# Attention's output split in place, and two out-projection blocks begun with it in the attention's PSUM banks

## The chip, the cores and the metric

The kernel runs on one core of one Trainium2 chip. The metric is the device time of one execution in microseconds; the median of three runs of the kernel before is 1607.62 us (1607.45 to 1609.95). Engines are named as in the profile: PE is TensorE, with PEld its weight loads, DVE is VectorE, ACT is ScalarE, POOL is GpSimd and SP is SyncE, whose only work here is to issue DMAs. L319 is line 319 of the kernel before.

## The reference, cut to what matters

One layer of a diffusion backbone over 1024 latent tokens (a grid 64 wide), 256 context tokens and model width 1024. Two groups of heads run side by side, and one projection joins them:

```python
px = modulate(rms_norm(x, norm1_w), sh1, sc1) @ w_in
# group A: gated DeltaNet, 4 heads of 128; chunked scans forwards and backwards, 
#          then per-head rms norm * silu(z)
dn_x, _, _ = gated_deltanet(px[..., :DN_IN], ..., s_ctx_f, s_ctx_b)
# group B: 8 heads of 64; softmax over an 8 x 16 window of keys and all context keys,
#          with a learned position bias
na_x = neighborhood_attention(qx, kx, vx, kc, vc, na_rpb, rows)
x = x + g1 * (jnp.concatenate([dn_x, na_x], axis=-1) @ w_out)
x = x + g2 * swiglu(modulate(rms_norm(x, norm2_w), sh2, sc2), w_ffn_in, w_ffn_out)
```

The concatenation matters for the change: the 1024 rows of `w_out` fall into 512 that meet group A's output and 512 that meet group B's, so a product over all of them can be begun with either half.

## The kernel before, in words

Numbers are held as pairs: an fp32 value is a `hi` (cast to the matmul's fp32r form) and a `lo` (the value less `hi`), and a product is three matmuls, hi by hi, lo by hi, hi by lo. Each operand is thus made by a cast on ACT and a subtraction on DVE or POOL. A scheduler sets the order of the instructions on each engine ahead of time, from the program's priorities and the life of its buffers, so the rows of an engine do not follow the lines of the source. An engine takes its rows in order; SP too, so a DMA that waits for its data or its buffer holds all DMAs behind it.

The kernel has four stages. The first, up to about 610 us, projects the input (L389) and prepares the chunk matrices of the scans. The second interleaves scans and attention. `scan` (L1085 to L1137) takes one of 10 chunks of 128 tokens in one direction: matmuls with the state (L1092, L1102), with `y` (L1111), with `at` (L1123) and `kt` (L1128), and DVE and ACT work on `vn`, `oacc`, `vk` in between. Its operands are loaded by `load` at L1065 to L1073, a chunk ahead, into three slots each. Where both directions have passed a chunk, `finish` norms it (L1149 to L1156), transposes it (L1161) and writes group A's part of the operand, `gah` and `gal` (L1164, L1165). Behind every step of a scan, `beside` advances `attention` by 0.72 of a step.

`attention` (L247 to L354) goes through 32 units, 4 pairs of heads by 2 halves of the rows by 4 blocks of columns. A unit takes a PSUM tile `sc` (1536 columns, two of them in turn) and goes: scores (L295), bias and maximum on DVE (L297), exponential on ACT (L300), scaling on DVE (L302), transposes (L307), copy to `pt` on ACT (L310), product with the values (L317), and a copy of the 128x128 result on ACT into `no` (L319). Four units fill a `no` tile, which SP stores in `na_d` in DRAM (L357).

The third stage is the out-projection (L1315 to L1376). `na_d` is read back (L1322) in four tiles of 512 KB, cast on ACT (L1325) and split on DVE (L1326) into `na`. With group A's `gah` and `gal` that makes the operand `parts`, eight pieces of 128 rows. Each of 8 blocks of 128 output columns takes 512 KB of `w_out` (`load_w`: DMA L197, cast L198, split L199), and 48 matmuls of 512 columns (L1349): eight pieces by three products by two halves of the tokens, the pieces of group A first. DVE then adds the result to the residual `x2` (L1334), whose input is loaded at L1344. The weights of block 0 are loaded during the scans already. Beside the blocks runs the background work `late`, the second half of the modulation (16 loads `wad` of 256 KB, L212, each with a DVE step L231 or L233); blocks 6 and 7 go together, at L1371. The fourth stage is the FFN, whose `Stream` loads the first 8 weight tiles `wq` (L1251, 256 KB each) when it is made, ahead of the out-projection, and casts and splits them (L1279, L1280).

Of the kernel before, what the change touches and what calls it, by code (L numbers as in the profile page):

```python
# [20 lines left out]
KT = 8  # L21
# [66 lines left out]
def hybrid(ctx, tc, a, dbg):  # L88
# [62 lines left out]
    vw_d = dram.tile([128, 4, 4, 512], F32, name="vw_d", tag="vw_d")  # L151
    na_d = dram.tile([4, 128, L], F32, name="na_d", tag="na_d")
    y_d = dram.tile([2, NCH, 128, 4, 128], F32, name="y_d", tag="y_d")
# [87 lines left out]

    hs = [slice(h * 128, h * 128 + 128) for h in range(4)]
    attn = ctx.enter_context(ExitStack())
    psum = []

    def attention(nw):
# [31 lines left out]
        def pair(heads, bts, vw, vc, half, cb, out):  # L278
# [34 lines left out]
            for j in range(5):  # L313
                for u, (w0, pt) in enumerate(zip(WIN, pts)):
# [3 lines left out]
                              start=j == 0, stop=j == 4)  # L318
            act.copy(out.rearrange("p (r b c) -> p r b c", r=8, b=4)[:, :, cb],  # L319
                     sc[:, 1280:1408].rearrange("p (r c) -> p r c", r=8))  # L320
            yield 1
# [7 lines left out]
        for n, (hp, half, cb) in enumerate(order):  # L329
            if half == 1 and cb in (0, 2) and hp + 1 < NAH // 2:  # L330
                heads.setdefault(hp + 1, []).append(load(2 * hp + 2 + cb // 2))
                if cb == 0:
                    vcs[hp + 1] = context(hp + 1)
            if cb == 0:
                out = nw.tile([128, 512], F32, name="no", tag="no")
            if old:
                next(old)
            cur = pair(heads[hp], bt, vw, vcs[hp], half, cb, out)
            next(cur)
            if n + 1 < len(order):  # L340
                bt, vw = biases(*order[n + 1]), values(*order[n + 1])
            yield 1
            if old:
                next(old)
                if cb == 0:
                    store(*done)
            if cb == 3:
                done = out, hp, half
            old = cur
            yield 1  # L350
        next(old)
        yield 1
        next(old)
        store(*done)  # L354

    def store(out, hp, half):
        sp.dma_start(na_d[hp, :, half * 512:half * 512 + 512], out)  # L357


    with ExitStack() as bs:  # L360
# [613 lines left out]
        for n in range(2, len(jobs) + 2):  # L974
# [8 lines left out]
            if n == len(jobs) - 1:  # L983
                bg.drain()
                late.close()
                fill = attention(pools(attn, "nw", "left", 2))
                next(fill)
# [52 lines left out]
    ga = [arp.tile([128, 4, L], F32R, name=n, tag=n) for n in ("gah", "gal")]  # L1040

    with ExitStack() as gs:
        sp1 = pools(gs, "sp1", "right")
# [3 lines left out]
        ps = gs.enter_context(tc.tile_pool(name="psg", bufs=1, space=PSUM))  # L1047
        psum.append(ps)
# [122 lines left out]
        def beside(n):  # L1171
            count[0] += n
            while count[0] >= 1:
                count[0] -= 1
                next(fill, 0)

        for d in range(2):
            load(d, ORDER[d][0])
        for i in range(NCH):
            if i + 1 < NCH:  # L1180
                for d in range(2):
                    load(d, ORDER[d][i + 1])
            live = [scan(d, ORDER[d][i]) for d in range(2)]
            while live:
# [11 lines left out]
    middle.close()  # L1196
    load_w = weights(wp)
    shift(ctx, "pad", "left", 8)
# [7 lines left out]
    rs = nrm.tile([128, L], F32, name="rs", tag="rs")  # L1206
    ps = ctx.enter_context(tc.tile_pool(name="psf", bufs=8, space=PSUM))

    def bank(name="ps"):
        return ps.tile([128, 512], F32, name=name, tag="ps")  # L1210

# [104 lines left out]
    with ExitStack() as os_:  # L1316
        nap = pools(os_, "nap", "right")
        nxt = load_w(a["w_out"][0], lo_engine=dve)
        na = []
        for k in range(4):  # L1320
            raw = wp.tile([128, KT, 132], F32, name="wraw", tag="wraw", bufs=2)[:, :, :128]
            sp.dma_start(raw, na_d[k].rearrange("p (i t) -> p i t", t=128))  # L1322
            n = nap.tile([128, 2, L], F32R, name=f"na{k}", tag=f"na{k}")
            n8 = n.rearrange("p h (i t) -> p h i t", t=128)
            act.copy(n8[:, 0], raw)  # L1325
            dve.tensor_tensor(n8[:, 1], raw, n8[:, 0].bitcast(F32), OP.subtract)  # L1326
            na.append(n)
        parts = [[x[:, k] for k in range(4)] + [n[:, i] for n in na] for i, x in enumerate(ga)]
        late = Background()
# [11 lines left out]

        for b in range(KT - 2):
            w, nxt = nxt, load_w(a["w_out"][b + 1], lo_engine=dve)
            sp.dma_start(x2[:, b], a["xcT"][b, :, CT:])  # L1344
            outs = [bank(), bank()]
            for k in range(KT):
                for j, (wi, xi) in enumerate(((0, 0), (0, 1), (1, 0))):
                    for o, s in zip(outs, HV):
                        pe.matmul(o, w[wi][:, k], parts[xi][k][:, s], start=k == 0 and j == 0,  # L1349
                                  stop=k == KT - 1 and j == 2)  # L1350
                if b and k % 2:
                    late.step()
# [293 lines left out]
```

## Time and profile before

| | |
|---|---|
| median of 3 runs | 1607.62 us (1607.45 to 1609.95) |
| the profiled execution's own time | 1608.33 us |
| its span | 1606.5 us |
| mean granted clock of PE | 0.982 |
| PE busy | 1504.8 us (94%) |
| DVE busy | 1037.5 us (65%) |
| ACT busy | 713.9 us (44%) |
| POOL busy | 201.2 us (13%) |
| mean transfer rate | 171 GB/s |

The span reaches from the first to the last instruction of the profiled execution; its own time has 1.8 us more around it. Busy time is that of instructions of an engine; waiting and issuing DMAs isn't counted. A releaser in brackets, as `[2.59 <-ACT whi L198]`, says how long the engine was idle ahead of a row and what ended that. The clock that the throttle granted to PE is given by stretch as a share of full speed. An SPq row is the time that SP needs to issue a DMA, not the transfer.

### The profile page before, as it was taken

How to read it: one execution, taken by the hardware profiler on the slowest of the kernel's cores; microseconds unless marked ns; L12 is line 12 of the kernel's file. 1: busy time of each engine (PE TensorE's matmuls, PEld its weight loads, DVE VectorE, ACT ScalarE, POOL GpSimd, SP SyncE). 2: the span in 40 equal slices, each digit the busy share in tenths (PEclk: the TensorE clock that was granted, in tenths of full speed). 3: DMA queues.
4: the chain of work that ended last, by engine and by line, in shares of the span. 5: the costliest groups of instructions: out<-in, count | busy, mean ns of one | idle time of the engine just before them, and what ended most of it. 6: DMA issues, size and time to landing. Idle time of an engine off the chain costs nothing.

```text
span 1606.5 us, 24016 instructions
## 1 busy us (share of the span) xinstructions
PE 1504.8 (94%) x8594; PEld 1265.4 (79%) x8594; DVE 1037.5 (65%) x1934; ACT 713.9 (44%) x1348; POOL 201.2 (13%) x275
## 2 busy tenths in 40 slices
PE   3999899899999998998997999999999999999999
PEld 1689788678888876787785887888888888888887
DVE  5866588445365665677897449865665655679752
ACT  5342452664434316666674147333333333544441
POOL 2053600512243310000000000000000000000000
PEclk9999999999999998999998999999999999999999
DMA  9366133535545348999846811532232333698742
GB/s 371 125 198 204 57 91 139 181 102 164 164 134 185 99 133 252 284 299 284 247 147 201 277 40 40 190 105 99 103 108 101 116 108 112 229 368 298 260 153 85
DMA packets 211529, 275.23 MB, mean 171 GB/s; under 512 B 15953, under 2 KB 119889, under 8 KB 210385
## 3 DMA queue, kind: packets, MB, share of 16 engines
q1 hardware_dynamic: 210544, 273.06, 52.2%
q8 instruction: 68, 1.11, 0.3%
q10 hardware_dynamic: 864, 0.63, 0.1%
q14 instruction: 53, 0.43, 0.1%
HBM read 206.78 MB, written 71.04 MB: 173 GB/s over the span
## 4 chain that ended last, share of the span: by engine, by line
PE 75%; DVE 7%; DMA 7%; ACT 5%; issue 3%; POOL 2%; SPq 1%; ACTq 0%; DVEq 0%; POOLq 0%
PE ps L1218 26%; PE ps L1565 13%; PE blk L389 10%; PE ps L1349 3%; PE blk L572 3%; PE pr L919 3%; PE sc L317 3%; PE sc L307 2%; PE sc L295 2%; PE pr L910 1%; PE ps L1111 1%; DVE tt L824 1%; PE ps L1371 1%; DMA nv_d<-zt 1%; DMA fraw<-w_conv 1%
## 5 line engine op out<-in xcount | busy, mean ns | idle before, releaser
L389 PE MATMUL blk<-hh,whi 128*128 128x512 f32 (+1 forms) x416 | 125.4, 394 | 4.1 <-ACT whi L198 1.6
L1279 ACT CAST uhi<-ws 128x512 fp32r<-128x512 f32 x91 | 54.7, 622 | 151.2 <-PE ps L1218 76.8
L1279 ACT CAST uhi<-wq 128x512 fp32r<-128x512 f32 x101 | 60.6, 621 | 135.9 <-issue 61.3
L389 PE MATMUL blk<-hh,wlo 128*128 128x512 f32 (+1 forms) x416 | 117.8, 377 | 2.3 <-POOL wlo L199 2.3
L389 PE MATMUL blk<-hl,whi 128*128 128x512 f32 (+1 forms) x416 | 115.5, 375 | 0.0
L1280 DVE TENSOR_TENSOR ulo<-wq,uhi 128x512 fp32r<-128x512 f32 x101 | 67.5, 688 | 66.9 <-ACT uhi L1279 36.9
L1218 PE MATMUL ps<-hT,uhi 128*128 128x512 f32 x336 | 104.3, 392 | 3.1 <-ACT hT L1397 3.1
L1218 PE MATMUL ps<-lT,uhi 128*128 128x512 f32 x336 | 103.6, 390 | 0.0
L1218 PE MATMUL ps<-hT,ulo 128*128 128x512 f32 x336 | 103.5, 389 | 0.0
L1218 PE MATMUL ps<-hB,uhi 128*128 128x512 f32 x288 | 89.7, 392 | 0.0
L1218 PE MATMUL ps<-lB,uhi 128*128 128x512 f32 x288 | 89.2, 391 | 0.0
L1218 PE MATMUL ps<-hB,ulo 128*128 128x512 f32 x288 | 88.9, 389 | 0.0
L389 PEld LDWEIGHTS blk<-hh,wlo 128*128 128x128 f32 x416 | 73.1, 191 | 18.3 <-POOL wlo L199 2.9
L389 PEld LDWEIGHTS blk<-hh,whi 128*128 128x128 f32 x416 | 71.6, 195 | 18.9 <-issue 3.2
L1280 DVE TENSOR_TENSOR ulo<-ws,uhi 128x512 fp32r<-128x512 f32 x91 | 60.8, 687 | 37.5 <-ACT uhi L1279 29.2
L389 PEld LDWEIGHTS blk<-hl,whi 128*128 128x128 f32 x416 | 73.4, 192 | 13.6 <-DVE hl L689 0.3
L572 PE MATMUL blk<-zhi,hh 128*128 128x264 f32 (+1 forms) x288 | 83.9, 291 | 0.0
L572 PE MATMUL blk<-zhi,hl 128*128 128x264 f32 (+1 forms) x288 | 82.1, 285 | 0.0
L572 PE MATMUL blk<-zlo,hh 128*128 128x264 f32 (+1 forms) x288 | 81.7, 284 | 0.0
L198 ACT CAST whi<-wraw 128x1024 fp32r<-128x1024 f32 x26 | 27.3, 1049 | 121.0 <-PE blk L389 50.3
L1218 PEld LDWEIGHTS ps<-hT,uhi 128*128 128x128 f32 x336 | 63.1, 189 | 16.4 <-ACT hT L1397 3.5
L1218 PEld LDWEIGHTS ps<-lT,uhi 128*128 128x128 f32 x336 | 63.4, 189 | 13.2
(333 smaller groups left out, 3738.5 us busy)
## 6 DMA issues: line engine op xcount, KB each, us to landing
wq<-w_fo SPq DMA_DIRECT2D x99, 256.0 KB
wq<-w_gu SPq DMA_DIRECT2D x88, 256.0 KB
wad<-wa SPq DMA_DIRECT2D x64, 256.0 KB
bt<-rpb SPq DMA_DIRECT2D x64, 192.0 KB
t_d<-g SPq DMA_DIRECT2D x22, 512.0 KB
fr<-t_d SPq DMA_DIRECT2D x44, 256.0 KB
f_d<-g SPq DMA_DIRECT2D x33, 256.0 KB
fr<-f_d SPq DMA_DIRECT2D x33, 256.0 KB
```

The costliest lines, as they stand in the source:

```text
L198: act.copy(h, r)
L295: pe.matmul(sc[:, u * 640 + n0:u * 640 + n1], q, ks[i], start=i == 0, stop=i == 1)
L307: pe.transpose(sc[:, u * 640 + j * 128:u * 640 + (j + 1) * 128], bt[:, j * 128:(j + 1) * 128], ident)
L317: pe.matmul(sc[u * ND:u * ND + ND, 1280:1408], vv, pt[:, j * 128:(j + 1) * 128], start=j == 0, stop=j == 4)
L389: pe.matmul(o, ww[:, k], xx[k][:, s], start=k == 0 and j == 0, stop=k == KT - 1 and j == end)
L572: pe.matmul(p[:, :c1 - c0], x[k][:, s], ww[:, k, c0:c1], start=k == 0 and j == 0, stop=k == KT - 1 and j == 2)
L919: pe.matmul(p[:, hs[h]], f[:, h], src[:, h], start=True, stop=True)
L1218: pe.matmul(o, w[wi][:, k], x[xi][:, k], start=first and k == 0 and j == 0, stop=k == n - 1 and j == 2, skip_group_check=True)
L1279: act.copy(hi, self.raw[key])
L1280: dve.tensor_tensor(lo, self.raw[key], hi.bitcast(F32), OP.subtract)
L1349: pe.matmul(o, w[wi][:, k], parts[xi][k][:, s], start=k == 0 and j == 0, stop=k == KT - 1 and j == 2)
L1565: pe.matmul(o[b], w[wi][:, b], F[xn, p][xi], start=n in (0, 1, 5) and p == 0 and j == 0, stop=p == NFB // 2 - 1 and j == 2, skip_group_che ...
```

## The change

Three things are changed.

1. `na_d`, its stores and its reloads are gone. The operand `na` (four tiles of two halves by 1024 columns, hi and lo) is allocated ahead of the scans, and each attention unit writes its result into it: hi by the ACT copy that was there, lo by a new DVE instruction that reads the PSUM tile.
2. The weight pool of the out-projection is opened after the scans instead of before them, so that block 0's weights are no longer loaded during the scans. The pools of the scans are stacked in another order.
3. `two_blocks` loads the second halves (the rows of group B) of the weights of blocks 0 and 1 in the last chunk, into slots that the scans' loads have left, casts them on ACT and splits them on POOL. It takes two attention PSUM tiles and puts 48 matmuls there, 24 of each block. After four rounds of the last chunk the rest of attention is issued, then 36 of these 48; the other 12 come behind the scans. The out-projection finishes blocks 0 and 1 with the first halves of their weights (24 matmuls each), and goes on with blocks 2 to 7 as before. The PSUM pool of the later stages is opened behind block 1.

```diff
-            act.copy(out.rearrange("p (r b c) -> p r b c", r=8, b=4)[:, :, cb],
-                     sc[:, 1280:1408].rearrange("p (r c) -> p r c", r=8))
+            hi, lo = (out[:, i, half * 512:half * 512 + 512].rearrange("p (r b c) -> p r b c", r=8, b=4)[:, :, cb]
+                      for i in range(2))
+            o = sc[:, 1280:1408].rearrange("p (r c) -> p r c", r=8)
+            act.copy(hi, o)
+            dve.tensor_tensor(lo, o, hi.bitcast(F32), OP.subtract)
...
-            cur = pair(heads[hp], bt, vw, vcs[hp], half, cb, out)
+            cur = pair(heads[hp], bt, vw, vcs[hp], half, cb, na[hp])
...
-    def store(out, hp, half):
-        sp.dma_start(na_d[hp, :, half * 512:half * 512 + 512], out)
...
-    wp = pools(stream, "wpf", "right", 2)
+    nap = pools(stream, "nap", "right")
+    na += [nap.tile([128, 2, L], F32R, name=f"na{k}", tag=f"na{k}") for k in range(4)]
...
+        def two_blocks():
+
+            tags = iter(("kT", "kt", "y", "qT", "at"))
+            piece = lambda dt: sl.tile([128, 4, 128], dt, name="ew", tag=next(tags))
+            raws = [piece(F32) for _ in range(2)]
+            for b, r in enumerate(raws):
+                sp.dma_start(r, a["w_out"][b, :, 4:])
+            ws = []
+            for b, r in enumerate(raws):
+                hi = piece(F32R)
+                lo = piece(F32R) if b == 0 else fw.tile([128, 4, 128], F32R, name="ew", tag="ew", bufs=1)
+                act.copy(hi, r)
+                pool.tensor_tensor(lo, r, hi.bitcast(F32), OP.subtract)
+                ws.append((hi, lo))
+            yield 1
+            for _ in range(2):
+                s = ps.tile([128, 1536], F32, name="sc", tag="sc", bufs=2)
+                begun.append([s[:, :512], s[:, 512:1024]])
+            for k in range(4):
+                for j, (wi, xi) in enumerate(((0, 0), (0, 1), (1, 0))):
+                    for w, outs in zip(ws, begun):
+                        for o, t in zip(outs, HV):
+                            pe.matmul(o, w[wi][:, k], parts[xi][4 + k][:, t], start=k == 0 and j == 0, stop=False,
+                                      skip_group_check=True)
+                    yield 1
...
+                rounds += 1
+                if i == NCH - 1 and rounds == 4:
+                    for _ in fill:
+                        pass
+                    for _ in range(9):
+                        next(begin)
-        for _ in fill:
+        for _ in begin:
             pass
...
+    wp = pools(stream, "wpf", "right", 2)
     load_w = weights(wp)
...
-        nxt = load_w(a["w_out"][0], lo_engine=dve)
+        ws = [load_w(a["w_out"][b, :, :4], kt=4, lo_engine=dve) for b in range(2)]
...
+        for b in range(2):
+            sp.dma_start(x2[:, b], a["xcT"][b, :, CT:])
+        for b, (w, outs) in enumerate(zip(ws, begun)):
+            for k in range(4):
+                for j, (wi, xi) in enumerate(((0, 0), (0, 1), (1, 0))):
+                    for o, s in zip(outs, HV):
+                        pe.matmul(o, w[wi][:, k], parts[xi][k][:, s], start=False, stop=k == 3 and j == 2,
+                                  skip_group_check=True)
+                if b and k % 2:
+                    late.step()
+            for p, s in zip(outs, HV):
+                add(b, s, p)
+            sp.dma_start(x2_d[b], x2[:, b])
+            if b == 0:
+                nxt = load_w(a["w_out"][2], lo_engine=dve)
+        scopes.close()
+        ps = ctx.enter_context(tc.tile_pool(name="psf", bufs=8, space=PSUM))
+        for b in range(2, KT - 2):
-        for b in range(KT - 2):
```

How it moves the rows of the engines is shown at three places. The first is the queue of SP where the scans begin. `v_d` and `nq_d` are stores of the first stage that the scans and the attention read back; `kT`, `v`, `y` and `kt` are the first loads of the scans, `qs`, `kh`, `kl` and `vc` those of attention's second head pair. Before:

```order
L519 DMA v_d<-vt 128x10x128
L252 DMA qs<-nq_d 128x1024
L254 DMA kh<-nk_d 64x1280
L255 DMA kl<-nk_d 64x1280
L254 DMA kh<-nk_d 64x1280
L255 DMA kl<-nk_d 64x1280
L197 DMA wraw<-w_out 128x8x128
L502 DMA nq_d<-hl_5147 64x1024 x4
L264 DMA bt<-rpb 128x384 x2
L1065 DMA kT<-kT_d 128x4x128
L1066 DMA v<-v_d 128x512
L1067 DMA y<-y_d 128x512
```

And after:

```order
L512 DMA v_d<-vt 128x10x128
L1062 DMA kT<-kT_d 128x4x128
L1064 DMA y<-y_d 128x512
L1065 DMA kt<-k_d 128x512
L1062 DMA kT<-kT_d 128x4x128
L1064 DMA y<-y_d 128x512
L1065 DMA kt<-k_d 128x512
L1062 DMA kT<-kT_d 128x4x128
L495 DMA nq_d<-hl_5146 64x1024 x4
L1062 DMA kT<-kT_d 128x4x128
L264 DMA bt<-rpb 128x384
L1063 DMA v<-v_d 128x512 x3
```

The loads of the second head pair and of `w_out` have left this place, and the scans' loads stand ahead of the last store of the first stage, but for `v`, whose slot lies over the data of that store.

The second place is PE in the last round of the scans, up to the out-projection. L307 and L317 are attention's, L1123 (L1120 after) and L1161 (L1158) the scans', L1349 and L1372 the out-projection's, L1196 the begun matmuls; `na_5178` to `na_5181` are the four tiles. Before:

```order
L307 MATMUL sc<-cst,bt 128x128 x5
L1111 MATMUL ps<-vn,y 128x128 x2
L1123 MATMUL ps<-vn,at 128x128 x2
L317 MATMUL sc<-pt,vc 64x128
L317 MATMUL sc<-pt,vw 64x128
...
L1123 MATMUL ps<-vn,at 128x128 x6
L1161 MATMUL ps<-cst,oacc 128x128 x8
L1349 MATMUL ps<-gah,whi 128x512 x2
L1349 MATMUL ps<-gal,whi 128x512 x2
```

And after:

```order
L1196 MATMUL sc<-na_5178,ew 128x512 x2
L307 MATMUL sc<-cst,bt 128x128 x5
L1120 MATMUL ps<-vn,at 128x128 x4
...
L1120 MATMUL ps<-vn,at 128x128 x4
L1196 MATMUL sc<-na_5178,ew 128x512 x8
L1196 MATMUL sc<-na_5179,ew 128x512 x12
L1196 MATMUL sc<-na_5180,ew 128x512 x12
L1158 MATMUL ps<-cst,oacc 128x128 x8
L1196 MATMUL sc<-na_5181,ew 128x512 x12
L1372 MATMUL sc<-gah,whi 128x512 x2
L1372 MATMUL sc<-gal,whi 128x512 x2
```

32 begun matmuls stand between the scans' last matmuls and the last transposes, 4 are strewn among the rows ahead, and 12 stand behind the transposes.

The third place is SP at the same point. Before:

```order
L264 DMA bt<-rpb 128x384
L357 DMA na_d<-no 128x512
L1344 DMA x_8357<-xcT 128x1024 x2
L1251 DMA wq<-w_gu 128x512 x8
L1322 DMA wraw<-na_d 128x8x128 x2
L212 DMA wad<-wa 128x512 x4
L197 DMA wraw<-w_out 128x8x128 x2
```

And after:

```order
L264 DMA bt<-rpb 128x384
L196 DMA wraw<-w_out 128x4x128
L1286 DMA wq<-w_gu 128x512 x8
L196 DMA wraw<-w_out 128x4x128
L1367 DMA x_8444<-xcT 128x1024 x2
L196 DMA wraw<-w_out 128x8x128
L211 DMA wad<-wa 128x512
```

Block 0's first half of `w_out` is issued ahead of the eight `wq` loads, block 1's behind them, then the residual's input for both blocks, block 2's weights and the modulation's.

More of the change, by code (lines that the diff above doesn't have):

```diff
@@ L985, in hybrid @@
                 late.close()
-                fill = attention(pools(attn, "nw", "left", 2))
+                fw = pools(attn, "nw", "left", 2)
+                fill = attention(fw)
                 next(fill)
@@ L1206, in hybrid @@
     rs = nrm.tile([128, L], F32, name="rs", tag="rs")
-    ps = ctx.enter_context(tc.tile_pool(name="psf", bufs=8, space=PSUM))
     def bank(name="ps"):
-        return ps.tile([128, 512], F32, name=name, tag="ps")
+        return ps.tile([128, 512], F32, name=name, tag="ps", bufs=2 if ps is psum[-1] else 8)
     def product(outs, ws, x, first=True):
@@ L1350, in hybrid @@
                                   stop=k == KT - 1 and j == 2)
-                if b and k % 2:
+                if k % 2:
                     late.step()
```

32 lines of the change are left out of this document (11 added, 21 removed).

## The prediction

> **What bounds the kernel now.** I read the page first, then the busy time by stage, then the timeline of TensorE and of what it waits for at the two ends of the scan stage, which are the places that the change touches.
>
> ```profile
> span 1606.5 us, 24016 instructions
> ...
> PE 1504.8 (94%) x8594; PEld 1265.4 (79%) x8594; DVE 1037.5 (65%) x1934; ACT 713.9 (44%) x1348; POOL 201.2 (13%) x275
> ...
> PE 75%; DVE 7%; DMA 7%; ACT 5%; issue 3%; POOL 2%; SPq 1%; ACTq 0%; DVEq 0%; POOLq 0%
> ```
>
> TensorE (PE) is busy 94% of the span and carries 75% of the chain that ended last. The change keeps its matmuls: the same 48 per block of out-projection, the same attention, the same scans. So it can only win where PE idles, or runs at a lowered clock, and the whole idle time is 1606.5 − 1504.8 = 101.7 us. The busy time by stage (columns: stretch, its length, busy of PE, of its weight loads, of DVE, ACT and POOL, then granted clock, DMA share, GB/s) shows how much of that lies at the change:
>
> ```profile
> 612.00:619.90 7.90, 2.36 (x17) 1.43 (x16) 5.12 (x13) 6.28 (x10) 0.00 (x0) 0.84 1.04 261
> 619.90:632.20 12.30, 10.75 (x57) 7.68 (x56) 6.04 (x16) 6.14 (x12) 1.54 (x4) 0.55 0.70 207
> 760.00:780.00 20.00, 16.98 (x148) 13.85 (x148) 17.60 (x77) 12.01 (x25) 1.87 (x6) 0.91 0.97 276
> 780.00:800.00 20.00, 18.47 (x170) 15.60 (x170) 18.05 (x76) 14.14 (x43) 1.87 (x6) 1.00 0.80 241
> 851.70:879.13 27.43, 16.83 (x57) 11.88 (x56) 20.66 (x56) 12.61 (x30) 0.00 (x0) 0.81 0.77 237
> ```
>
> At the start of the scans PE idles 5.5 us in the first stretch and 1.6 us in the second, which besides runs at a clock of 0.55. At the end of the scans it idles 27.43 − 16.83 = 10.6 us. In the second half of the scans (the rows at 760 and 780) PE is near full and VectorE (DVE) is busy 88 and 90% of the time: there DVE has no slack to speak of. Now PE's timeline from the last scan matmul on (start, duration, instruction, count, and in brackets the idle time ahead with its releaser):
>
> ```profile
> 850.11 1.60 PE L1123 MATMUL ps<-vn,at 128*128 128x128 f32 x12
> ...
> 858.60 1.17 PE L1161 MATMUL ps<-cst,oacc 128*128 128x128 f32 x4 [1.25 <-DVE oacc L1156]
> 861.33 1.22 PE L1349 MATMUL ps<-gah,whi 128*128 128x512 f32 x2 [1.56 <-DVE gal L1165]
> ...
> 866.61 0.62 PE L1349 MATMUL ps<-gah,whi 128*128 128x512 f32 x2
> 867.07 0.61 PE L1349 MATMUL ps<-gal,whi 128*128 128x512 f32 x2
> ...
> 879.13 0.72 PE L1349 MATMUL ps<-gah,whi 128*128 128x512 f32 x2 [2.59 <-ACT whi L198]
> ...
> 892.04 0.62 PE L1349 MATMUL ps<-gah,whi 128*128 128x512 f32 x2
> ```
>
> The scans' last matmul ends at 851.7. PE then waits for the output norm on DVE, does the last transposes, and starts block 0 of the out-projection at 861.33, slowly: six pairs from 861.33 to 866.61, 0.88 us each, against 0.46 from 866.61 to 867.07. Block 1 starts at 879.13 after a wait for its weights, and block 2 at 892.04.
>
> **The change part by part.** *The hole at the end of the scans.* The 48 begun matmuls (24 pairs) put 24 × 0.46 = 11.0 us of the two blocks' work ahead of gah and gal. 36 of them stand ahead of the last transposes, 12 behind; a few go into waits of the last chunk, and some 32 follow the last scan matmul: 16 × 0.46 = 7.4 us, so 851.7 to about 859.1. The first 36 need only na0 to na2, which are written long before. PE stays busy there, so I take the full clock. Transposes then end at about 861 (859.77 now), the 12 others at 863.7, and gah and gal are there by then (861.3 now). Block 0's other 24 matmuls have their weights early, 12 × 0.46 = 5.5, so it ends at 869.2. Its hi/lo split of the weights costs nothing there, as ACT and DVE have been idle for it; without that cover it would be the 0.6 and 0.7 us of a 128x512 cast and split.
>
> Block 1 is where it stalls. Its first-half weights are issued behind eight wq loads, which wait for the last transposes:
>
> ```profile
> 859.80 4.36 SPq L1251 DMA_DIRECT2D wq<-w_gu  x8
> ```
>
> What landed behind them in the kernel before shows on ACT, which casts what has come (8 wq and the third of the na tiles by 871.29, the fourth by 872.99):
>
> ```profile
> 866.59 1.96 ACT L1279 CAST uhi<-wq 128x512 fp32r<-128x512 f32 x3 [1.17 <-DMA wq<-w_gu]
> 871.29 1.05 ACT L1325 CAST na<-wraw 128x1024 fp32r<-128x1024 f32 x1 [2.74 <-DMA wraw<-na_d]
> 872.99 1.05 ACT L1325 CAST na<-wraw 128x1024 fp32r<-128x1024 f32 x1 [0.65 <-DMA wraw<-na_d]
> 878.04 1.04 ACT L198 CAST whi<-wraw 128x1024 fp32r<-128x1024 f32 x1 [4.00 <-DMA wraw<-w_out]
> ```
>
> 512 KB took 1.7 us. The ninth 256 KB would have come at 871.29 − 0.85 = 870.4; all is 1.2 us later with the transposes, so 871.6, and 872.2 with a 0.6 us cast. PE waits 869.2 to 872.2, 3.0 us, and block 1's 24 matmuls end at 877.7 at full clock. Next late is block 2, whose PSUM banks lie over the scans' and so wait for block 1's eviction on DVE, in whose queue stands:
>
> ```profile
> 873.67 0.49 DVE L231 TENSOR_SCALAR acc<-wad,sc 128x512 f32<-128x512 f32 x1
> ...
> 877.45 1.40 DVE L1334 SCALAR_TENSOR_TENSOR x<-ps,modp,x 128x512 f32<-128x512 f32 x2
> 879.12 1.23 DVE L199 TENSOR_TENSOR wlo<-wraw,whi 128x1024 fp32r<-128x1024 f32 x1 [0.26 <-ACT whi L198]
> ```
>
> the first modulation step (waits its wad load), the split of block 2's weights, then two evictions. Behind the ninth load come 2 × 512 KB of x, 512 KB of w_out and 256 KB of wad: 871.6 + 3 × 1.7 = 876.7 for w_out, 0.9 more for wad, 877.6; then 0.49 + 1.23 + 1.40 gives 880.7, and block 2 starts at about 881. Against 892.04 that is 11.0 us won, less what the clock takes: after a 2.59 us stall, block 1 of now took 892.04 − 879.13 = 12.9 for 24 × 0.46 = 11.0 us of work, 1.9 lost. Two stalls of about 3 us lie in my sequence, but if block 1 is slowed, the second one shrinks. I take 1.0 lost: **−10 us**, between −6 (both stalls 2 us longer) and −12.5 (neither lowers the clock, and w_out comes 1.5 us earlier).
>
> [...]
>
> *The start of the scans.* The w_out load of 512 KB and the second head pair's loads leave the stretch ahead of the first scan loads:
>
> ```profile
> 614.85 0.59 SPq L197 DMA_DIRECT2D wraw<-w_out  x1
> ...
> 624.85 0.64 SPq L1065 DMA_DIRECT2D kT<-kT_d  x1
> ```
>
> ```profile
> 632.16 1.16 PE L1111 MATMUL ps<-v,y 128*128 128x128 f32 x8
> ```
>
> The scans' first matmul now comes at 632.16, 7.3 us behind the first load; after the change it stands 17 rows earlier in PE's order. There kT, y and kt of four pieces are issued ahead of nq_d, and only v waits for that store to land. The bound is the 7.1 us idle in the first two stretches (nothing gained to all of it); v can hardly be there before 626 or 627, so I take 4 to 5 us earlier, and **−4 us**. The queue also loses 8 na_d stores (2 MB), two of four na_d reloads at the end are no longer in front of anything, and 0.5 MB of w_out: at 276 GB/s some 9 us of transfers in a stage where the DMA share is 0.80 to 0.97. PE's waits there are for engines, not for DMA, mostly, so I count nothing, and keep 8 us for a rival.
>
> *The price in the scans.* Each of 32 attention units gets one more DVE instruction, out of PSUM and a 128x128 tile, and its PSUM tile is released by DVE, behind ACT. Nearest rows: a DVE instruction of 128x128 with PSUM input, and ACT's copy of this very piece.
>
> ```profile
> L1105 DVE SCALAR_TENSOR_TENSOR oacc<-ps,EG,oacc 128x128 f32<-128x128 f32 x32 | 9.3, 344 | 1.1 <-PE ps L1102 1.0
> ...
> L319 ACT COPY no<-sc 128x128 f32<-128x128 f32 x31 | 8.3, 269 | 14.6 <-PE sc L317 14.3
> ```
>
> 9.3 / 32 = 0.29 us each, so 32 × 0.29 = 9.3 us of DVE. (Bounds: 0.27, ACT's copy of the same piece, to 0.34, the mean length of one: 8.6 to 11 us; I take 0.29, of the same engine and size in a row of four.) Half of them lie where DVE is 90% busy, 4.6 us, and half of those where DVE, not PE, ends last: **+2 us**, between 0 and +9. Behind a waiting lo on DVE stand the scans' vn and oacc and the softmax, for which PE waits. PE's wait for that release is small so far:
>
> ```profile
> PE sc L295 <- ACT no L319: 1.6, 5, 0.4
> ```
>
> It gets longer by about 0.3 us a time. The splits of the begun blocks' weights go to POOL:
>
> ```profile
> L886 POOL TENSOR_TENSOR rg<-GL,cst 128x512 fp32r<-128x512 f32 x20 | 21.8, 1089 | 0.0
> ```
>
> two of 1.09 us, well ahead of their use, on an engine busy 1.87 of 20 us there: nothing. [...]
>
> *The rest.* Four casts of na on ACT (1.05) and four splits on DVE (1.22) go; the tail behind block 2 has the same order on PE, and PE fills it: nothing.
>
> Sum: −10 − 4 + 2 = −12 us. Against the profiled execution's 1608.33 (span 1606.5) this is 1596.3; the median of the runs shown, 1607.62, lies 0.7 below it: **1595.6 us**. A measurement of this kernel can tell about 0.2%, 3.2 us, from no change.
>
> **The rivals.** (A) *Half the gain*: the weights of blocks 1 and 2 come 2 us later each than I have them, since more loads share the engines (−10 + 4 = −6), and the scans' start gains nothing, as PE waits for v all the same (0); with the price of +2 that is −4, 1604.3 in the profiled execution, 1603.6 as a median. For it: the clock of 0.55 and the DMA share of 1.04 at the start; against: PE's order. (B) *Slower*: lo holds up both the PSUM tile and the scan's recurrence. If each of 32 units costs 0.29 and a wait for hi of 0.27 (ACT's copy) on PE's path, 18 us are lost; against −14 from the ends that is +4 (17.9 − 14), 1611.6. It decides from 14 / 32 = 0.44 us a unit. For it: DVE's 88 to 90%; against: PE is as full there, and two PSUM tiles alternate. (C) *DMA sets the scans' pace*: 2.5 MB less gives 6 us beyond my sum, 1589.6. For it: shares of 0.97; against: PE's waits. (D) *The clock stays full* behind both stalls: the 1.0 us that I took off for it isn't lost, 1594.6. For it: the stalls are short; against: the slow pairs behind 879.13. [...] (E) *The change doesn't do what it says*: the begun matmuls wait themselves (weights `ew` late, or the last lo), PE idles as now, and the 9 us of lo stand against the gain at the start: no change.
>
> **How the numbers follow.** Chances: my forecast 0.53, A 0.14, B 0.06, C 0.11, D 0.10, E 0.06. Faster by over 0.2% are the forecast, C, D and most of A (0.11), together 0.85; same are 0.03 of A and 0.05 of E, 0.08; slower are B and 0.01 of E, 0.07. Range: from C with a better transition (−12.5 − 4 − 4 = −20.5, 1587.1; I take 1588) to A's 1603.6. B, E and the outer part of A are left out, some 0.17.
>
> **What would show it.** Right: in the changed profile PE's first begun matmuls fill 852 to 859; a stall of about 3 us stands ahead of block 1 (released by ACT whi) and one ahead of block 2 (released by DVE x); block 2 starts 12 to 13 us earlier in the span than 892; the first scan matmul stands near 628; the lo instruction takes near 0.29. Wrong: the window from 640 to 850 grows by over 6 us, with PE waiting for the lo line or for vn; or block 2's start is not earlier relative to the last scan matmul; or the FFN, whose loads start later now, begins to wait.

## The result, and the profile after

The changed kernel takes 1599.1 us in the median of four runs (1597.69 to 1602.98), against 1607.81 of the kernel before beside it. The ratio is 0.9948, with a 95% interval of 0.9931 to 0.9966. That is 8 to 9 us won, where 12 were forecast: the sign and the range were right, and the time lies 3.5 us above the 1595.6 of the forecast. A second set of six runs gave 1599.3 us and 0.9951 (0.9931 to 0.9970). The profiled execution has 1595.9 us of span against 1606.5.

```profile
span 1595.9 us, 24024 instructions
...
PE 1500.9 (94%) x8594; PEld 1263.5 (79%) x8594; DVE 1039.0 (65%) x1962; ACT 709.4 (44%) x1346; POOL 204.4 (13%) x277
```

PE has its 8594 matmuls as before, DVE 28 instructions more (32 for lo, less four for the old split). The end of the scans in PE's timeline (start, duration, count, idle time ahead):

```profile
853.73 1.16 PE L1120 MATMUL ps<-vn,at 128*128 128x128 f32 x8
854.64 7.61 PE L1196 MATMUL sc<-na,ew 128*128 128x512 f32 x32
862.10 1.04 PE L1158 MATMUL ps<-cst,oacc 128*128 128x128 f32 x8
862.89 3.02 PE L1196 MATMUL sc<-na,ew 128*128 128x512 f32 x12
865.74 0.62 PE L1372 MATMUL sc<-gah,whi 128*128 128x512 f32 x2
...
873.28 0.73 PE L1372 MATMUL sc<-gah,whi 128*128 128x512 f32 x2 [1.92 <-ACT whi L197]
...
881.37 0.70 PE L1390 MATMUL ps<-gah,whi 128*128 128x512 f32 x2 [2.34 <-ACT ws L1363]
881.91 0.62 PE L1390 MATMUL ps<-gal,whi 128*128 128x512 f32 x2
882.37 0.62 PE L1390 MATMUL ps<-gah,wlo 128*128 128x512 f32 x2
```

The reader is to see the hole filled: 32 begun matmuls run in 7.6 us where PE waited for the output norm, 12 more follow the transposes, and two stalls are left, 1.92 us for block 1's weights and 2.34 us ahead of block 2. From the last scan matmul (854.9) to block 2 it is 26.5 us, against 40.3 (851.7 to 892.0) before: 13.8 less. DVE's timeline says what the second stall is:

```profile
878.17 0.48 DVE L230 TENSOR_SCALAR acc<-wad,sc 128x512 f32<-128x512 f32 x1 [2.07 <-DMA wad<-wa]
878.67 1.23 DVE L198 TENSOR_TENSOR wlo<-wraw,whi 128x1024 fp32r<-128x1024 f32 x1
879.82 1.40 DVE L1358 SCALAR_TENSOR_TENSOR x<-sc,modp,x 128x512 f32<-128x512 f32 x2
```

It is the chain that was forecast: the modulation step waits for its load, the split of block 2's weights and block 1's eviction stand behind it, and PE starts when the eviction ends, at 881.2. The profile names ACT for this wait; DVE is what ended it.

In the scans, the lo instruction costs what was forecast, and DVE stays as full:

```profile
L323 DVE TENSOR_TENSOR na<-sc,na 128x128 fp32r<-128x128 f32 x32 | 9.1, 284 | 3.2 <-ACT na L322 2.9
```

```profile
760.00:780.00 20.00, 17.23 (x160) 14.25 (x161) 18.20 (x78) 11.63 (x25) 1.87 (x6) 1.00 0.70 197
780.00:800.00 20.00, 16.82 (x154) 13.89 (x153) 17.53 (x75) 14.19 (x43) 2.15 (x6) 1.00 0.68 193
```

These are the stretches at 760 and 780 of the busy time by stage. PE's busy time fell between 780 and 800, from 18.47 to 16.82 us, and the DMA share from 0.80 to 0.68: the transfers that are gone were not what held PE.

Since the runs of one kernel lie up to 8 us apart (those of the kernel before up to 11), the experiments are read by stage, from one profiled execution each. The first attention matmul (L295) stands at 612.2 to 620.8 in them, 613.2 before and 614.4 after, though the first stage is the same program; so all stretches are counted from there on. Each ratio is to runs of the kernel before beside that kernel, whose medians are 1607.81 to 1609.58. Times in us:

| kernel | first attention matmul to last scan matmul | from there to blocks 6 and 7 | median of runs | ratio to before, interval |
|---|---|---|---|---|
| before | 238.5 | 85.6 | 1607.81 | 1 |
| changed kernel | 240.5 | 71.9 | 1599.1 | 0.9948 (0.9931 to 0.9966) |
| changed, again | 240.2 | 72.9 | 1599.3 | 0.9951 (0.9931 to 0.9970) |
| no_lo | 235.8 | 73.9 | 1596.97 | 0.9918 (0.9899 to 0.9938) |
| lo2 | 242.5 | 71.2 | 1601.49 | 0.9955 (0.9941 to 0.9969) |
| in_place_only | 240.6 | 81.0 | 1608.2 | 0.9995 (0.9985 to 1.0006) |
| lo_pool | 238.1 | 73.5 | 1598.46 | 0.9923 (0.9906 to 0.9939) |
| early_wx | 241.0 | 75.4 | 1603.14 | 0.9963 (0.9949 to 0.9977) |
| b2bank | 240.9 | 71.7 | 1602.36 | 0.9952 (0.9936 to 0.9969) |
| early_wx_b2 | 240.5 | 77.0 | 1604.58 | 0.9975 (0.9963 to 0.9987) |
| wq_late | 240.6 | 73.0 | 1600.55 | 0.9940 (0.9924 to 0.9957) |
| wq_late_psf | 241.0 | 72.1 | 1602.41 | 0.9954 (0.9938 to 0.9970) |
| all3 | 240.2 | 74.6 | 1600.4 | 0.9940 (0.9922 to 0.9957) |
| before_wq_late | 235.8 | 81.2 | 1603.07 | 0.9966 (0.9952 to 0.9979) |

Where the begun matmuls are there, a few are strewn into the last chunk and lengthen the first stretch by 0.23 us each: four in most kernels (0.9 us), three in lo2, and only one in no_lo, lo_pool and all3. Profiles in which the scans are the same program differ by up to 0.8 us in this stretch (240.2 to 241.0).

### The profile page after: what moved, and what is told of

Read it like the earlier page. It is cut to its first block, busy times and chain, and to the rows that moved or that the text cites. A ratio compares the mean times of both kernels' runs of the same rounds, so it can differ in the third digit from the quotient of the medians.

```text
span 1595.9 us, 24024 instructions
## 1 busy us (share of the span) xinstructions
PE 1500.9 (94%) x8594; PEld 1263.5 (79%) x8594; DVE 1039.0 (65%) x1962; ACT 709.4 (44%) x1346; POOL 204.4 (13%) x277
## 4 chain that ended last, share of the span: by engine, by line
PE 46%; DVE 2%; ACT 1%; DMA 1%; issue 0%; SPq 0%; ACTq 0%; DVEq 0%
PE ps L1253 26%; PE ps L1606 13%; PE ps L1390 3%; PE ps L1412 1%; PE sc L317 1%; PE sc L307 1%; DMA wad<-wa 1%; PE sc L1196 1%; DVE x L1445 0%; PE ps L1120 0%; DVE bt L297 0%; DMA wq<-w_gu 0%; PE sc L295 0%; PE ps L1089 0%; PE ps L1099 0%
## 5 line engine op out<-in xcount | busy, mean ns | idle before, releaser
L197 ACT CAST whi<-wraw 128x1024 fp32r<-128x1024 f32 (+1 forms) x26 | 26.4, 1017 | 109.9 <-PE blk L382 50.1
```

Of the source, the lines that this page charges most:

```text
L197: act.copy(h, r)
```

## The experiments

**The changed kernel again**, as a base.

> The changed kernel as it is, beside the others, as their base. Its four times so far lie between 1597.7 and 1603.0 us, so 1597.5 to 1601 as a median, 7 to 10 us under the kernel before. In its profile the stretch from the first attention matmul (L295) to the last scan matmul (L1120) should take about 240 us, and that from there to block 2 about 27 us.

It came as said, 240.2 us of scans and 27.6 us from there to block 2. But one thing differs from the first profile: block 1's stall is 2.17 us here, and the pairs behind it run slowly.

```profile
871.04 1.22 PE L1372 MATMUL sc<-gah,whi 128*128 128x512 f32 x2 [2.17 <-ACT whi L197]
872.06 1.06 PE L1372 MATMUL sc<-gal,whi 128*128 128x512 f32 x2
```

The clock records show the difference. In each profile every lowered period begins and ends on one grid of 3.41 us, and is one to four of these steps long (3.41 to 13.65 us before, 3.41 and 6.83 in the first profile of the changed kernel), at a clock of 0.50. Here are the step that holds most of the stall and the one behind it (length, busy time of each engine with PE first, then clock, DMA share and GB/s), from this profile:

```profile
867.53:870.95 3.42, 1.34 (x6) 0.76 (x5) 1.51 (x3) 1.82 (x3) 0.00 (x0) 1.00 1.04 369
870.95:874.36 3.41, 3.32 (x8) 2.67 (x9) 2.10 (x3) 1.06 (x3) 0.00 (x0) 0.50 0.99 318
```

And the same two steps from the first profile of the changed kernel:

```profile
869.69:873.10 3.41, 1.67 (x8) 1.05 (x6) 1.81 (x3) 1.74 (x3) 0.00 (x0) 1.00 1.04 383
873.10:876.51 3.41, 3.23 (x14) 2.69 (x15) 2.10 (x3) 1.14 (x3) 0.00 (x0) 1.00 1.03 327
```

PE was idle for 61% of the one step and 51% of the other, and only behind the first did the clock fall. Between 580 and 940 us of all 14 profiles, a full clock fell behind each of the 31 steps in which PE idled 54% or more (in the profile of before these are steps of 56, 67, 67 and 95%, in the first of the changed kernel one of 100%), and stayed behind each of the 1389 with less than 50%; of the four in between one fell. It is not the whole rule: elsewhere in these profiles 11 falls came behind steps with less than 50%, one of 33% at 156 us of the changed kernel, and from 3 to 20 us of both kernels' first profiles PE is wholly idle at a clock of 1.00.

**What does lo cost?** In no_lo the DVE instruction is left out, and the lo halves are zeroed once:

```diff
             act.copy(hi, o)
-            dve.tensor_tensor(lo, o, hi.bitcast(F32), OP.subtract)
...
+    for n in na:
+        pool.memset(n[:, 1].bitcast(F32), 0.0)
```

> Leaves out attention's lo: the 32 new DVE instructions (L323) are gone and the lo halves of na are set to zero once, ahead of the scans, so that the output lacks the product with them; all matmuls stay. Theory 1, that the gain forecast for the scans is eaten by these instructions where DVE is the bound (9.1 us of DVE in the profile, half of them in the second half of the scans): 4 to 6 us faster than the changed kernel, nearly all of it between 740 and 855 us. Rival, that the new order of the scans and of attention's loads costs it (the DVE work there is the same, only moved): within 1.5 us of the changed kernel.

In lo2 the line stands twice.

> Each of the 32 lo instructions is issued twice. Theory 1: another 5 to 8 us slower than the changed kernel, about 1605, as the doubled ones stand behind one another where DVE is the bound. Rival (order, not the instructions): under 2 us slower. If PE's wait for the PSUM tile is what costs, it shows as waits of L295 for L323, and the doubling costs 9 us or more.

Without lo the scans take 235.8 us, 4.4 to 4.7 less than with it. Of that, 0.7 us are the three begun matmuls that have moved behind the scans here, so that some 4 us stay with lo. The ratio falls from 0.9951 to 0.9918, 5 us (the medians lie 2.3 us apart), though the two intervals overlap. Theory 1 said 4 to 6. The place is mostly as it said. To see it, one follows an instruction that every chunk has, `vn` behind L1111 (L1114 after, L1115 in no_lo), on DVE's timeline. Here are the ninth and the fifteenth of its 16, first in the changed kernel:

```profile
747.56 0.69 DVE L1114 TENSOR_TENSOR vn<-ps,NB 128x512 f32<-128x512 f32 x1
...
848.27 0.68 DVE L1114 TENSOR_TENSOR vn<-ps,NB 128x512 f32<-128x512 f32 x1
```

and in no_lo:

```profile
749.84 0.69 DVE L1115 TENSOR_TENSOR vn<-ps,NB 128x512 f32<-128x512 f32 x1
...
847.39 0.67 DVE L1115 TENSOR_TENSOR vn<-ps,NB 128x512 f32<-128x512 f32 x1
```

The first attention matmuls stand at 614.37 and 617.75, so the two are 133.2 and 233.9 us behind it with lo, 132.1 and 229.6 without: 1.1 and 4.3 us apart. A quarter of the price falls ahead of the ninth, three quarters behind it, where DVE is some 90% busy. But lo2 speaks only half for the theory: 9.0 us of DVE more cost 2.0 to 2.3 us of scans and 2.2 us of the median, not 5 to 8, which is nearer the rival's "under 2 us".

```profile
L323 DVE TENSOR_TENSOR na<-sc,na 128x128 fp32r<-128x128 f32 x32 | 9.1, 285 | 3.0 <-ACT na L322 2.7
L324 DVE TENSOR_TENSOR na<-sc,na 128x128 fp32r<-128x128 f32 x32 | 9.0, 282 | 0.2
```

The second copy waits 0.2 us in all, the first 3.0, nearly all for ACT's hi. So the price is not one of DVE's seconds alone; what the first one adds and a second doesn't, the wait for hi and the order that the scheduler makes of it, can be in it. How it divides stays open, since the rows of the scans stand in another order in no_lo than in the changed kernel, and in lo2 in yet another.

**Lo on POOL.** ACT copies the result in fp32 into a tile of four units, casts it at the end, and POOL subtracts:

```diff
-            act.copy(hi, o)
-            dve.tensor_tensor(lo, o, hi.bitcast(F32), OP.subtract)
+            act.copy(out.rearrange("p (r b c) -> p r b c", r=8, b=4)[:, :, cb], o)
...
+    def halves(out, hp, half):
+        hi, lo = (na[hp][:, i, half * 512:half * 512 + 512] for i in range(2))
+        act.copy(hi, out)
+        pool.tensor_tensor(lo, out, hi.bitcast(F32), OP.subtract)
```

> The lo instructions leave DVE: ACT copies each unit's result in full fp32 into a tile of four units, as in the kernel before, and then ACT casts the 128x512 tile to hi and POOL makes lo, 8 times each instead of 32 DVE instructions. Nothing is left out. Theory 1 (the 9.1 us of lo on DVE cost about 5 us of the scans): the stretch from the first attention matmul to the last scan matmul comes down from 240.4 to 235 to 237 us, and the time by 3 to 5 us. Rival, that POOL and DVE hold each other up when both read SBUF: under 2 us gained, with the same DVE rows longer than now (L297 822 ns, L302 557 ns, L1102 342 ns).

The scans take 238.1 us, 2.2 less, of which 0.7 is begun work as in no_lo: less than half of what no_lo gives, and 1 us short of the expectation. Apart from lo, the rows of DVE take as long as in the changed kernel but for one:

```profile
L302 DVE TENSOR_SCALAR bt<-bt,mx 128x640 f32<-128x640 f32 x64 | 37.2, 581 | 0.5
...
L359 POOL TENSOR_TENSOR na<-no,na 128x512 fp32r<-128x512 f32 x8 | 10.5, 1308 | 33.6 <-ACT na L358 33.6
```

L302 took 35.6 us, 557 ns each, in the changed kernel. The mean hides what happens: two of the 64 ran into a subtraction on POOL and took 1.54 and 1.56 us, where the median is 548 ns. One of them, with POOL's row:

```profile
773.46 1.54 DVE L302 TENSOR_SCALAR bt<-bt,mx 128x640 f32<-128x640 f32 x1
773.38 1.26 POOL L359 TENSOR_TENSOR na<-no,na 128x512 fp32r<-128x512 f32 x1 [4.14 <-ACT na L358]
```

That is 2.0 us of DVE, the rival on a small scale, and about what the scans take longer than in no_lo (2.3 us), whose order is nearly the same; L297 stays at 822 ns. Ahead of block 2 there is a stall of 2.12 us here, no longer than in the changed kernel, and yet the clock falls behind it (PE was busy for 1.41 of the 3.41 us from 880.12 on), which takes 1.6 us of the gain again:

```profile
882.12 0.70 PE L1399 MATMUL ps<-gah,whi 128*128 128x512 f32 x2 [2.12 <-ACT ws L1372]
...
883.61 1.05 PE L1399 MATMUL ps<-gah,whi 128*128 128x512 f32 x2
884.46 1.05 PE L1399 MATMUL ps<-gal,whi 128*128 128x512 f32 x2
```

With 0.9923 (0.9906 to 0.9939) this is the fastest of the kernels that compute everything, but not clear of the changed kernel's interval.

**Without the begun blocks.** two_blocks is left out, and all blocks go through the loop as before:

```diff
-                begin = two_blocks()
-                next(begin)
...
-        for b in range(2, KT - 2):
+        for b in range(KT - 2):
```

> The split in place without the begun blocks: two_blocks is left out, and all 8 blocks go as before, the weights of block 0 coming after the scans. Theory 1, that the begun blocks carry the gain by filling PE at the end of the scans (PE idle 10.6 us there before, 5.2 us after): the gain goes whole, 11 to 15 us slower than the changed kernel, 1610 to 1614, since the weights of block 0 then come late too. Rival, that the way through DRAM was what made the hole and its removal pays by itself: 1600 to 1605.

The whole gain goes: ratio 0.9995, within 0.2% of no change, 9 us slower than the changed kernel, somewhat less than theory 1 said. The waits for the norm are there again, and no lighter:

```profile
860.97 1.17 PE L1158 MATMUL ps<-cst,oacc 128*128 128x128 f32 x4 [3.91 <-DVE oacc L1153]
866.19 1.17 PE L1158 MATMUL ps<-cst,oacc 128*128 128x128 f32 x4 [4.04 <-DVE oacc L1153]
868.92 1.22 PE L1339 MATMUL ps<-gah,whi 128*128 128x512 f32 x2 [1.56 <-DVE gal L1162]
```

The stretch behind the scans is 4.6 us shorter than before (81.0 for 85.6), but lo costs the scans about as much. So the way past DRAM has no net gain by itself; it is what lets the blocks begin.

**The two stalls that are left.** Three kernels tried to remove them. In early_wx the first halves of the weights and the residual's input are issued ahead of the wq loads; in b2bank block 2 takes the scans' two banks, and the later pool opens behind it; early_wx_b2 has both:

```diff
+    ws = [load_w(a["w_out"][b, :, :4], kt=4, lo_engine=dve) for b in range(2)]
+    for b in range(2):
+        sp.dma_start(x2[:, b], a["xcT"][b, :, CT:])
     up = Stream()
...
-        scopes.close()
-        ps = ctx.enter_context(tc.tile_pool(name="psf", bufs=8, space=PSUM))
         for b in range(2, KT - 2):
+            if b == 3:
+                scopes.close()
+                ps = ctx.enter_context(tc.tile_pool(name="psf", bufs=8, space=PSUM))
```

> The first halves of the weights of both blocks and the residual's input for both are issued ahead of the eight wq loads. If the loads' place is what holds block 1, its stall of 1.9 us (ACT whi) goes; the stall ahead of block 2 (2.3 us) goes or shrinks by up to 2 us, since only block 2's weights and the modulation's load stand behind wq then. The stretch from the last scan matmul to block 2 falls from about 27 to 23 to 25 us. Rival: the wait only moves to block 2's weights, whose load still follows the wq loads; then the stretch falls by less than 1 us.

> Only the PSUM banks of block 2 are changed: it takes the two banks of the scans, which are free by then, so that it doesn't wait for block 1's eviction. If the eviction is what holds block 2, its stall of 2.3 us shrinks to what its weights need: the split of its weights on DVE ended at 879.9 where block 2 began at 881.4, so 1.0 to 1.5 us less. Rival: weights arrive with it, no change.

> Both of the two edits above together. If the two stalls are what is left of the hole, the stretch from the last scan matmul to block 2 falls from about 27 to 22 to 24 us, and the time by 3 to 5 us; by the rival (block 2's weights behind wq decide alone) by 1 to 2 us.

None is faster. In early_wx block 1's stall is gone, and all of it comes back ahead of block 2:

```profile
885.41 1.22 PE L1390 MATMUL ps<-gah,whi 128*128 128x512 f32 x2 [5.72 <-DVE acc L230]
886.43 1.05 PE L1390 MATMUL ps<-gal,whi 128*128 128x512 f32 x2
887.28 1.05 PE L1390 MATMUL ps<-gah,wlo 128*128 128x512 f32 x2
```

And one stall of 5.72 us costs more than 1.92 and 2.34 apart: the pairs behind it run at 0.85 us each until 889.8, those behind the two short ones of the first profile at 0.46. In b2bank block 2 follows block 1 at once, and block 3 waits 1.68 us for the pool:

```profile
884.52 0.73 PE L1391 MATMUL ps<-gah,whi 128*128 128x512 f32 x2
...
897.75 0.70 PE L1391 MATMUL ps<-gah,whi 128*128 128x512 f32 x2 [1.68 <-ACT ws L1363]
```

The stretch to blocks 6 and 7, 71.7 us, is as in the changed kernel. early_wx_b2 has a stall of 5.10 us and the least gain of the three, 0.9975, with an interval that only just overlaps that of the changed kernel.

**The wq loads later.** wq_late makes the FFN's stream behind block 2's weights; wq_late_psf also lets the later PSUM pool wait tile by tile; all3 adds lo on POOL:

```diff
-    up = Stream()
...
             if b == 0:
                 nxt = load_w(a["w_out"][2], lo_engine=dve)
+                up = Stream()
```

> The changed kernel, but the eight wq loads of the FFN are issued behind the weights of block 2 instead of ahead of block 1's. If the wq loads' place is what makes the two stalls: block 1's (1.9 us) and most of block 2's (2.3 us) go, the stretch from the last scan matmul to block 2 falls from about 27 to 23 to 24.5 us, with the full clock behind it; the time falls by 2.5 to 4 us. Rival, that the wait only moves on (to the eviction of block 1, or to block 3's weights behind the wq loads now): the stretch falls, but blocks 2 to 5, 45.4 us from the first matmul of block 2 to that of blocks 6 and 7, get longer by as much.

> As wq_late, and the later stages' PSUM pool waits tile by tile for what lies under it, so that block 2 may start when block 0's banks are free. If block 1's eviction is the last wait: another 1 to 1.5 us off the stretch, no stall left ahead of block 2, 22.5 to 23 us. Rival: no difference from wq_late within 0.5 us in the stretch.

> wq_late_psf with the lo of attention made on POOL in four-unit tiles. If the three terms add: the scans' stretch 238 us instead of 240.4, the stretch to block 2 at 23 us, together 5 to 7 us under the changed kernel, some 1592 to 1595 us. If they don't add (PE full at the end of the scans, or the loads collide), under 3 us.

The runs of none of the three are clear of the changed kernel's. Block 1's stall goes, and ahead of block 2 stands 4.14 us (wq_late). DVE shows why:

```profile
877.71 1.23 DVE L198 TENSOR_TENSOR wlo<-wraw,whi 128x1024 fp32r<-128x1024 f32 x1 [2.17 <-ACT whi L197]
878.85 1.29 DVE L1315 TENSOR_TENSOR ulo<-wq,uhi 128x512 fp32r<-128x512 f32 x2
880.31 1.90 DVE L1315 TENSOR_TENSOR ulo<-wq,uhi 128x512 fp32r<-128x512 f32 x3 [0.17 <-ACT uhi L1314]
882.12 1.40 DVE L1357 SCALAR_TENSOR_TENSOR x<-sc,modp,x 128x512 f32<-128x512 f32 x2
```

The splits of the wq tiles, which ran in the earlier wait while nobody needed DVE, now stand ahead of block 1's eviction, for which PE waits. In wq_late_psf block 2's first matmul runs at once, and the second waits 3.11 us for the same eviction. The three terms of all3 don't add either: behind the scans it has the same wait (3.99 us) and 74.6 us to blocks 6 and 7. Its scans run in the order of lo_pool's and yet take 240.2 us for 238.1; the busy time by stretches of 4 us shows a lowered clock there, which takes some 0.34 × 4 + 0.50 × 4 = 3.4 us at most:

```profile
760.00:764.00 4.00, 2.86 (x15) 2.52 (x15) 4.00 (x27) 2.58 (x7) 0.62 (x2) 0.66 0.70 154
764.00:768.00 4.00, 4.00 (x29) 3.46 (x28) 2.39 (x11) 1.92 (x5) 0.31 (x1) 0.50 0.59 181
```

**Was it the queue?** The same move in the kernel before:

```diff
-    up = Stream()
...
             sp.dma_start(x2[:, b], a["xcT"][b, :, CT:])
+            if b == 0:
+                up = Stream()
```

> The kernel before, with the wq loads made behind the first block's operands instead of ahead of them. It asks how much of the hole at the end of the scans was this queue and not the missing work. My theory: PE waits there for the output norm on DVE (4.5, 1.3 and 1.6 us), which no load shortens, so that at most block 1's stall of 2.6 us and part of its slow pairs go: 2 to 4 us faster than the kernel before, 12.5 us behind the gain of the begun blocks' stage. Rival, that the queue was the hole: 7 to 10 us faster.

```profile
855.06 1.17 PE L1161 MATMUL ps<-cst,oacc 128*128 128x128 f32 x4 [4.46 <-DVE oacc L1156]
857.49 1.17 PE L1161 MATMUL ps<-cst,oacc 128*128 128x128 f32 x4 [1.26 <-DVE oacc L1156]
860.22 1.22 PE L1350 MATMUL ps<-gah,whi 128*128 128x512 f32 x2 [1.56 <-DVE gal L1165]
...
873.74 0.73 PE L1350 MATMUL ps<-gah,whi 128*128 128x512 f32 x2 [0.42 <-ACT whi L198]
...
876.33 0.74 PE L1350 MATMUL ps<-gah,wlo 128*128 128x512 f32 x2 [1.39 <-DVE wlo L199]
```

The waits for the norm stay as they were within 0.01 us, as theory 1 said. Block 1's falls from 2.59 to 0.42 us, but two pairs later its lo weights bring another of 1.39; the stretch to blocks 6 and 7 is 4.4 us shorter. The runs gain more than the 2 to 4 us expected, 0.9966 (0.9952 to 0.9979), 5.5 us. So about two thirds of what the change won, by the interval 3.4 to 7.7 us of its 8, was to be had by issuing eight loads later; in the changed kernel the same move (wq_late) wins nothing clear. The other part of the difference is in its scans, 235.8 against 238.5 us, where its order is that of the kernel before but for the last rows. Of that, 1.7 us are a lowered clock in the profiled execution of before, which the changed kernel and before_wq_late do not show at that place:

```profile
760.00:764.00 4.00, 1.87 (x13) 1.25 (x13) 4.00 (x25) 2.31 (x5) 0.31 (x1) 1.00 1.08 325
764.00:768.00 4.00, 3.96 (x31) 3.21 (x29) 3.93 (x22) 2.13 (x5) 0.62 (x2) 0.57 1.03 229
```

PE idles 2.1 us to 764, and the clock behind it is 0.57 for 4 us: 0.43 × 4 = 1.7 us. In the changed kernel the same stretch has 1.8 us idle, and the clock stays full; in before_wq_late it has 2.4 us, spread over two steps of 3.41 us with 43 and 37% idle, and the clock stays full too. The other 1.0 us has no cause shown.

## Why the prediction was right, and where its size was off

- *The hole at the end of the scans, −10 forecast: the mechanism right, the size −12.3.* 13.8 us (with the second profile 12.7) lie between the last scan matmul and block 2, and 0.9 of the begun work lies ahead of that; −12.3 is the mean. The 32 matmuls took 7.6 us (7.4 forecast), the transposes ended 8.2 us behind the scans (9.3 forecast). The stalls were 1.92 and 2.34 us for 3.0 and 3.3 forecast. For the clock I took off 1.0. In the first profile it stayed full behind both stalls, which is rival D; in the second it fell for one step of 3.41 us behind block 1's, 2.17 us, and block 2's shrank to 1.60, as the forecast describes, and the stretch to block 2 is 1.1 us longer. So the 1.0 us is right for one of two executions, and which one comes was luck: the stalls differ by 0.25 us. The length alone doesn't tell the two apart. In this stage stalls of 2.12 (lo_pool), 2.17 and 2.38 us (no_lo) lowered the clock, as did 2.59 us before and all longer ones; those of 1.4 to 1.9 us and one of 2.34 did not. Nor was a wholly idle step needed: between 580 and 940 us steps of 3.41 us with PE idle for 54% of the time or more were enough (61% in after_again, 59% in lo_pool), and the clock behind them was 0.50.
- *The start of the scans, −4 forecast: wrong in size, next to nothing.* The first scan matmul came 14.5 us behind the first attention matmul, against 19.0: 4.5 us earlier, as the step said. But the step took that for a gain of the stage, and it was only an exchange of order: at the first `vn` the changed kernel is 4.6 us behind the kernel before (44.7 and 40.1 us), at the fifth 2.2 ahead (90.5 and 92.7). no_lo, the same start without lo, needs 235.5 us for the stretch without its one begun matmul, against 235.8 of before_wq_late, whose scans are those of before without the dip of the clock: 0.3 us won, less than the profiles differ. What counts is PE's idle time, and most of the 7.1 us at the start stayed: 4.35 and 1.38 us in the same two windows. Counted from the first attention matmul, which stands 1.2 us later here, they are 5.55 and 0.18 us: the long wait of attention in the first window is as it was.

```profile
612.00:619.90 7.90, 3.55 (x20) 1.90 (x19) 3.92 (x8) 6.43 (x8) 0.00 (x0) 1.00 1.06 320
619.90:632.20 12.30, 10.92 (x74) 8.80 (x73) 6.16 (x22) 7.96 (x21) 1.54 (x4) 0.72 0.84 258
```

- *The price in the scans, +2 forecast: +4.* The instruction takes 0.284 us as forecast (0.29), 9.1 us in all; the share of it that the scans grow by, taken as a quarter, is over two fifths (from 235.5 to 239.5 us, both without the begun work). The step that was mis-sized is "half of those where DVE, not PE, ends last". It stays inside the bounds of 0 to 9. That the same again costs only 2 us more says that the share isn't a constant, and as the order changes too, the 4 us are not shown to be DVE's alone.
- *The sum.* −12.3 − 0.3 + 4.0 = −8.6 us, and 8.0 to 8.7 were measured. That the forecast missed by no more than 3.5 us is in part luck: the hole gave 2.3 us more than it said, the two other terms 3.7 and 2.0 us less. The two profiled executions lie 10.6 us apart, since that of before holds the 1.7 us of lowered clock.
- *The rivals.* A had the start right, where it expected nothing, and the hole wrong; the result lies 3.5 us above my forecast and 4.5 below A's time. B did not come, since 4.0 / 32 = 0.125 us a unit is far below 0.44. C stands in the working with 8, 6 and 4 us; it is excluded, as the DMA share fell without PE gaining (0.97 to 0.70 between 760 and 780), and as no_lo, which has the transfers gone and no lo, wins 0.3 us in the scans. D came in one of two executions. E is excluded by in_place_only.

Still open is how the price of lo divides into DVE's time, the wait for hi, and the changed order, and what of the spread of the runs, up to 8 us in one kernel, is not the clock. In after_again the two slowest, 1603.9 and 1604.5 us, have mean clocks of 0.983 and 0.982, the fastest, 1596.3 us, has 0.988; but in no_lo runs of 1591.2 and 1596.0 us both have 0.987.

## What to carry to other kernels

Work that can be begun from one half of its operand fills a wait that no faster load shortens, and this is where the gain came from (0.9948, and 0.9995 without the begun blocks); keeping data out of DRAM was only what made it possible. An instruction that starts earlier is a gain only if the engine that bounds the stage idles less (the first scan matmul came 4.5 us earlier here, and the scans won 0.3), so look at its idle time and not at the first row. And before a stall is attacked, look at what the waiting engine's neighbours do in that time: in every attempt here the splits, loads or evictions that the stall had covered became the next one, of 1.68 us (b2bank) to 5.72 us (early_wx).

## What had not been expected of the hardware

A stall of 5.72 us (early_wx) cost another 2.4 us behind it: six pairs in 5.2 us (885.41 to 890.62) for 6 × 0.46. A stall need not be long to lower the clock: 2.17 us did in one execution of the changed kernel, 1.92 and 2.34 us did not in another; PE's idle share of a step of 3.41 us was 61% in the one and 51% in the other. At the clock of 0.50 each lowered step takes up to half of its 3.41 us, 1.7 us; that is a part of the spread of the runs, and a reason to compare stretches and not whole spans where 0.5% matters. POOL's subtraction of 128x512 took 1308 ns beside the scans (lo_pool, L359), and 1089 in the first stage of the kernel before (L886). A `tensor_scalar` of 128x640 on DVE that ran into one took 1.54 us for 0.55 (lo_pool, L302), while L297, which reads PSUM, kept its mean of 822 ns.
